# Starting the first layer with memory's keys and values, from inputs turned on the host

## The chip, the cores and the metric

One core of a Trainium2 chip runs the whole program. The time is device microseconds of one execution of the program; the verdict on a kernel is the median of several runs. Inputs are handed over once, ahead of the launch; what the host does to their layout is not in the time.

## What is computed

An encoder of two layers over 512 positions of width 2048, all in float32. Per layer, cut to what matters here:

```python
h = rmsnorm(x, pre_norm_g[l])                       # (512, 2048)
z = h @ w_in[l]                                     # combined input projection, split into columns:
q_lat, kv_lat, k_pe, gb, gc, xin, q_mem, gate = split_cols(z)
...                                                 # latent attention -> a_out, short convolution -> c_out
mem_n = rmsnorm(mem, mem_norm_g[l])                 # (256, 2048), the same mem in both layers
mk, mv = mem_n @ w_mk[l], mem_n @ w_mv[l]           # (256, 512) each: four heads of 128
m_out = softmax(q_mem @ mk^T * scale) @ mv
y = concat(a_out, c_out, m_out) * silu(gate)
x = x + rmsnorm(y @ w_o[l], post_norm_g[l])
```

`rmsnorm(v, g)` is `v * r * g` with one factor `r = (mean(v*v) + eps) ** -0.5` per row (per position, or per memory token) and one gain `g` per column.

## The kernel before

**Products.** Each float32 operand is split into a high half that the matmul format holds exactly and the rest (`split_to`, and `prep` for weights: ScalarE writes the high half, VectorE subtracts it from the source for the low one). `mm3` makes a product of three matmuls: high by high, high by low, low by high. The large projections go by one level of a seven-product scheme (P1 to P7): with the operand halves A11, A12 (token tiles 0 and 1) and A22, S1 to S4, which are made of all four token tiles (0 and 2, or 1 and 3). `left_half` splits A11 and A12 of a token tile; `right_half` puts off, one by one, A22's split and the sums and splits of S1, S2, S4, S3 (`combine`).

**Steps.** `Program` holds a list of steps, each with the weight units it needs. Ahead of a step, `load` issues the units' loads on SyncE's queue (up to eight units ahead, eight raw buffers) and `prep` splits them (two units ahead, three buffers of each half). `defer(cost, fn)` puts work off: every step brings some room, and the queue's head is emitted when its cost is there. `until` empties the queue as far as an operand is needed, all at once. So the program writes one order down, and each engine's instructions stand in that order; in the first part (`manual_schedule`, until `first.close`) VectorE and ScalarE take it literally, behind it the scheduler may reorder these two. TensorE, SyncE and GpSimd keep it throughout.

**Layer 0.** Four tiles of x (128 positions each) are loaded by rows. ScalarE squares and sums (`row_factor`), GpSimd makes the factor, VectorE multiplies it in (`first_rows`), TensorE turns the tile in 16 transposes of 128x128 (`transpose_rows`), and the eviction multiplies the column gain in. Sixty transposes of the identity (`warm`) fill TensorE before. The column gains are loaded by rows and turned with one transpose (`turn_constants`). The first projection group, HEAD, runs in the order P1, P2, P1' and P2' of the second group, P5, P6 with P3, and so on; P1 needs A11, P2 A12, P5 S1. Before P1's second weights come the second halves of the tiles, beside P2 the third and fourth tile.

**Memory in layer 0.** Rows of mem are loaded late in the projection, scaled by their row factor (`mem_rows`) and, in the mixer, turned by 32 transposes (`mem_turn`), split, and written to DRAM as split halves (`mTd`) for layer 1. `mem_steps` makes keys (`mk`, transposed: 128 columns by 256 tokens, four banks) and values (`mv`, tokens by 512 columns, two banks) in eight pairs of steps; the column gain of the memory norm is multiplied into the weights as they are split (`gain`, two pieces of 512 columns). They stand between the gates' transposes; the rotary tables are made beside them.

**Memory in layer 1.** `mem_steps` stands between the transposes at the start of the layer, with the halves reloaded from `mTd` (`mem_reload`); its keys and values go to DRAM and come back for the mixer (`mem_fetch`).

Of the kernel before, what the change touches and what calls it, by code (L numbers as in the profile page):

```python
# [5 lines left out]
F32 = mybir.dt.float32  # L6
F32R = mybir.dt.float32r
# [73 lines left out]
class Program:  # L81
# [36 lines left out]
    def run(self):  # L118
# [39 lines left out]
        def prep(upto):  # L158
            while at["prep"] < min(upto, len(seq)):
# [48 lines left out]
def encoder(tc, x, mem, positions, pre_norm_g, w_in, q_norm_g, w_uq, kv_norm_g, w_ukv, conv_w,  # L208
            mem_norm_g, w_mk, w_mv, w_o, post_norm_g, inv_freq, out):
# [61 lines left out]
    def setup():  # L271
# [11 lines left out]
        nc.scalar.dma_start(rows[2 * n:], conv_w.rearrange("l k (c p) -> (l k c) p", p=P))  # L283
        G["rows"] = rows

    def turn_constants():
        rows = G["rows"]
        n = KT * depth
        m = 2 * n + 12 * depth
        ps = bank("cps")  # L290
        nc.tensor.transpose(ps[:, :m], rows, G["ident"][:m, :m])
        cols = const.tile([P, m], F32, name="cols")
        nc.vector.tensor_copy(cols, ps[:, :m])
# [281 lines left out]
    def row_factor(xt, junk):  # L575
        ssq = small()
        nc.scalar.activation(junk, xt, AF.Square, accum_out=ssq)
        return rsqrt_mean(ssq, D)

    def normalise_rows(xt, dst, on=None):  # L580
        r = row_factor(xt, dst)
        if on is nc.scalar:
            nc.scalar.activation(dst, xt, AF.Copy, scale=r)
        else:
            nc.vector.tensor_scalar_mul(dst, xt, r)
# [29 lines left out]

    def first_load(t):
        xt = G[f"x{t}"] = slab("x")
        nc.sync.dma_start(xt, x[0, t * P:(t + 1) * P, :])

    def first_factor(t):  # L620
        G[f"hs{t}"] = slab("hs")
        G[f"r{t}"] = row_factor(G[f"x{t}"], G[f"hs{t}"])

    def first_rows(t, halves=(0, 1)):
        for h in halves:
            c = slice(h * 1024, (h + 1) * 1024)
            nc.vector.tensor_scalar_mul(G[f"hs{t}"][:, c], G[f"x{t}"][:, c], G[f"r{t}"])
# [820 lines left out]
```

## Time and profile before

| | |
|---|---|
| median of 3 runs | 1506.56 us (1505.59 to 1508.12) |
| span of the profiled execution | 1503.7 us; its own whole time isn't given apart from the runs' |
| TensorE (PE) busy | 1486.0 us, 7613 matmuls and transposes |
| VectorE (DVE) busy | 1082.5 us, 1444 instructions |
| ScalarE (ACT) busy | 873.5 us, 1359 instructions |
| first matmul of a projection | 14.64 us from the span's start |

In the profile's lines a name is that of a tile, `out<-in`; P is a bank of a projection, wh and wl are the halves of a weight unit, wr its raw buffer, A and S the left operands, hs scaled rows, hT a turned tile, mk and mv the banks of keys and values, mH and mL the halves of turned memory. "Lnnn" is the line of the kernel. A time in brackets is what the engine idled ahead of the group, with what ended it. A line of the windows has, for a stretch of the span, its length, the busy time of PE, of its weight loads (PEld), DVE, ACT and GpSimd (POOL), the granted clock, the DMA engines' busy share and GB/s. A line of the groups ends in count, busy us and mean ns of one.

### The profile page before, as it was taken

Reading aid. Unit: us, or ns where it says so; the run is one execution under the profiler, and the core shown is the slowest. Engines: PE = TensorE matmul, PEld = TensorE weight load, DVE = VectorE, ACT = ScalarE, POOL = GpSimd, SP = SyncE. Lnnn points to the kernel's source line nnn. Section 1 sums busy time; section 2 is a strip of 40 time slices with the busy share of each in tenths; the row PEclk is TensorE's granted clock in tenths of the full one; section 3 lists DMA queues with packets and bytes.
Section 4 is the critical chain, followed back from the end, with each engine's and each line's share of the span. In section 5 each row is a group of like instructions: output and inputs, shape, how many; then the busy total and the mean of one; then the engine's idle time right before and its main releaser. Section 6 shows DMA issues by size and latency. Waiting matters only on the chain.

```text
span 1503.7 us, 20253 instructions
## 1 busy us (share of the span) xinstructions
PE 1486.0 (99%) x7613; PEld 1279.1 (85%) x7613; DVE 1082.5 (72%) x1444; ACT 873.5 (58%) x1359; POOL 256.9 (17%) x253
## 2 busy tenths in 40 slices
PE   9999999999999999999999999999999999999997
PEld 7788888988898888888898888888988888988886
DVE  6965776575877668769788765776575486698687
ACT  7743434454767768655688533534464587686443
POOL 1233030322000000230310233030323000003211
PEclk9999999999999999999999999999999999999999
DMA  8999796979582111495987999696979521027945
GB/s 335 216 215 223 192 187 160 203 210 248 168 262 81 56 34 65 101 211 166 319 297 234 236 224 223 196 179 159 212 199 220 152 71 43 29 84 140 257 120 183
DMA packets 142581, 267.19 MB, mean 178 GB/s; under 512 B 17084, under 2 KB 39956, under 8 KB 139156
## 3 DMA queue, kind: packets, MB, share of 16 engines
q0 software_dynamic: 52544, 117.19, 39.7%
q1 hardware_dynamic: 89808, 148.67, 30.0%
q8 instruction: 59, 0.97, 0.3%
q14 instruction: 38, 0.31, 0.1%
q10 hardware_dynamic: 132, 0.05, 0.0%
HBM read 251.20 MB, written 14.68 MB: 177 GB/s over the span
## 4 chain that ended last, share of the span: by engine, by line
PE 93%; ACT 2%; DVE 1%; issue 1%; POOL 1%; DMA 1%; POOLq 0%; DVEq 0%; ACTq 0%
PE P L253 22%; PE P L254 22%; PE P L252 22%; PE ptp L1021 2%; PE tps L772 2%; PE o L253 1%; PE o L254 1%; PE o L252 1%; PE sc L252 1%; PE sc L253 1%; PE sc L254 1%; PE mk L253 1%; PE mk L254 1%; PE mk L252 1%; PE sc L1001 1%
## 5 line engine op out<-in xcount | busy, mean ns | idle before, releaser
L178 DVE TENSOR_TENSOR wl<-wr,wh 128x1024 fp32r<-128x1024 f32 (+1 forms) x400 | 476.9, 1196 | 283.0 <-ACT wh L177 274.5
L177 ACT CAST wh<-wr 128x1024 fp32r<-128x1024 f32 (+1 forms) x400 | 412.6, 1034 | 451.0 <-PE P L254 379.9
L252 PE MATMUL P<-wh,S 128*128 128x512 f32 (+1 forms) x896 | 345.2, 385 | 0.0
L253 PE MATMUL P<-wl,S 128*128 128x512 f32 (+1 forms) x896 | 343.9, 384 | 0.4 <-DVE wl L178 0.4
L254 PE MATMUL P<-wh,S 128*128 128x512 f32 (+1 forms) x896 | 343.3, 383 | 0.0
L252 PE MATMUL P<-wh,A 128*128 128x512 f32 (+1 forms) x656 | 253.1, 386 | 0.2 <-ACT wh L177 0.2
L253 PE MATMUL P<-wl,A 128*128 128x512 f32 (+1 forms) x656 | 251.9, 384 | 0.8 <-DVE wl L178 0.8
L254 PE MATMUL P<-wh,A 128*128 128x512 f32 (+1 forms) x656 | 251.7, 384 | 0.5 <-DVE A L258 0.5
L137 POOL DMA_DIRECT2D wr<-in_w_in_dram x136 | 164.6, 1210 | 460.2 <-DVE wl L178 284.5
L253 PEld LDWEIGHTS P<-wl,S 128*128 128x128 f32 x896 | 168.3, 188 | 30.7 <-DVE wl L178 1.2
L254 PEld LDWEIGHTS P<-wh,S 128*128 128x128 f32 x896 | 168.2, 188 | 30.4
L252 PEld LDWEIGHTS P<-wh,S 128*128 128x128 f32 x896 | 168.1, 188 | 29.6
L254 PEld LDWEIGHTS P<-wh,A 128*128 128x128 f32 x656 | 123.2, 188 | 23.3 <-DVE A L258 1.2
L253 PEld LDWEIGHTS P<-wl,A 128*128 128x128 f32 x656 | 123.2, 188 | 22.8 <-DVE wl L178 1.4
L252 PEld LDWEIGHTS P<-wh,A 128*128 128x128 f32 x656 | 123.1, 188 | 22.3 <-ACT wh L177 0.7
L137 POOL DMA_DIRECT2D wr<-in_w_o_dram x40 | 48.4, 1211 | 530.4 <-DVE wl L178 515.3
L1007 ACT ACTIVATE P<-sc,nm 128x512 f32<-128x512 f32 (+1 forms) x96 | 59.9, 623 | 31.1 <-DVE nm L1004 31.1
L1010 ACT ACTIVATE P<-P,rec 128x512 f32<-128x512 f32 (+1 forms) x96 | 63.2, 661 | 6.7 <-DVE rec L1009 6.7
L1004 DVE TENSOR_REDUCE nm<-sc 128x1 f32<-128x512 f32 (+1 forms) x96 | 57.3, 596 | 9.6 <-PE sc L1002 6.1
L258 DVE TENSOR_TENSOR PT<-ptp,PT 128x512 fp32r<-128x512 f32 (+1 forms) x96 | 55.0, 596 | 10.0 <-ACT PT L257 9.6
L183 DVE SCALAR_TENSOR_TENSOR wl<-wr,cols,wh 128x512 fp32r<-128x512 f32 x64 | 45.9, 750 | 13.5 <-ACT wh L182 13.5
L182 ACT ACTIVATE wh<-wr,cols 128x512 fp32r<-128x512 f32 x64 | 44.0, 726 | 19.2 <-PE mk L253 7.8
(281 smaller groups left out, 2238.7 us busy)
## 6 DMA issues: line engine op xcount, KB each, us to landing
wr<-in_w_in_dram SPq DMA_DIRECT2D x128, 512.0 KB, 5.5
wr<-in_w_in_dram POOLq DMA_DIRECT2D x112, 512.0 KB, 7.3
wr<-in_w_o_dram SPq DMA_DIRECT2D x48, 512.0 KB, 4.0
wr<-in_w_o_dram POOLq DMA_DIRECT2D x40, 512.0 KB, 7.0
wr<-in_w_in_dram SPq DMA_DIRECT2D x32, 416.0 KB, 4.0
wr<-in_w_in_dram POOLq DMA_DIRECT2D x24, 416.0 KB, 5.8
wr<-in_w_mk_dram SPq DMA_DIRECT2D x16, 512.0 KB, 5.7
wr<-in_w_mv_dram SPq DMA_DIRECT2D x16, 512.0 KB, 5.0
```

The costliest lines, as they stand in the source:

```text
L137: engine.dma_start(dst, src, **kw)
L177: nc.scalar.copy(hi[:, :n], src)
L178: nc.vector.tensor_tensor(lo[:, :n], src, hi[:, :n].bitcast(F32), op=ALU.subtract)
L182: nc.scalar.activation(hi[:, h], src[:, h], AF.Copy, scale=g)
L183: nc.vector.scalar_tensor_tensor(lo[:, h], src[:, h], g, hi[:, h].bitcast(F32), op0=ALU.mult, op1=ALU.subtract)
L252: nc.tensor.matmul(ps, ah, bh, start=first, stop=False, **kw)
L253: nc.tensor.matmul(ps, ah, bl, start=False, stop=False, **kw)
L254: nc.tensor.matmul(ps, al, bh, start=False, stop=last, **kw)
L258: nc.vector.tensor_tensor(lo, src, hi.bitcast(F32), op=ALU.subtract)
L1004: nc.vector.tensor_reduce(nmax, ps, axis=AX.X, op=ALU.max, negate=True)
L1007: nc.scalar.activation(pt, ps, AF.Exp, bias=nmax, accum_out=tot)
L1010: nc.scalar.activation(pt, pt, AF.Copy, scale=rec)
```

## The change

The host hands over x and mem a second time, turned (`xt` in tiles of 128 positions, `memt`), and all column gains in one turned table (`columns`). Layer 0 begins with the sixteen memory steps; memory's column gain is multiplied into turned memory as it is split (four pieces of 256 columns a unit), its row factor into keys (along the free side, by a row made with a broadcast and a transpose, `factor_row`) and values (by partition). The same is done in layer 1 with `memt` loaded again. x's rows are still loaded, for the row factors alone (`row_factors`); the turned tiles are scaled in place, sixteen instructions of 128x128 a tile (`turned_scale`). What stands beside which memory step is in `beside`. The third and fourth tile's turned loads come beside memory, their rows beside P2, and their scaling and both `right_half` go on the put-off queue behind P1' has begun. Keys and values of both layers go by DRAM to the mixer, which now is the same in both layers; the rotary tables come in the projection. Sixty warm-up transposes become thirty.

```diff
                 else:
-                    for k, g in enumerate(u.gain()):
-                        h = slice(k * (n // 2), (k + 1) * (n // 2))
+                    gains = u.gain()
+                    for k, g in enumerate(gains):
+                        h = slice(k * (n // len(gains)), (k + 1) * (n // len(gains)))
                         nc.scalar.activation(hi[:, h], src[:, h], AF.Copy, scale=g)
                         nc.vector.scalar_tensor_tensor(lo[:, h], src[:, h], g, hi[:, h].bitcast(F32),
                                                        op0=ALU.mult, op1=ALU.subtract)
...
         G.update(ident=identr.bitcast(F32), identr=identr, mhalf=mhalf, junk=const.tile([P, 512], mybir.dt.bfloat16, name="junk"))
-        rows = scrap("rows", P)[:KT * 2 * depth + 12 * depth]
         n = KT * depth
-        nc.scalar.dma_start(rows[:n], pre_norm_g.rearrange("l (k p) -> (l k) p", p=P))
-        nc.scalar.dma_start(rows[n:2 * n], mem_norm_g.rearrange("l (k p) -> (l k) p", p=P))
...
+        cols = const.tile([P, 2 * n + 12 * depth], F32, name="cols")
+        nc.scalar.dma_start(cols, columns)
...
+    def row_factors(key, src, t, dst):
+
+        def load():
+            G[key, t] = slab("rows")
+            nc.sync.dma_start(G[key, t], src[t * P:(t + 1) * P, :])
+
+        def factor():
+            rows = G.pop((key, t))
+            ssq = small()
+            nc.scalar.activation(rows, rows, AF.Square, accum_out=ssq)
+            ms = small(1, "ms")
+            nc.gpsimd.tensor_scalar(ms, ssq, 1.0 / D, EPS, op0=ALU.mult, op1=ALU.add)
+            nc.gpsimd.tensor_tensor(dst[:, t:t + 1], ms, G["mhalf"][:, :1], op=ALU.pow)
+        return load, factor
+
+    def factor_row(name, ts):
+
+        src = G[name]
+        dst = scrap("row", len(ts) * P)
+        G[name + "_row"] = dst.rearrange("p (t c) -> p t c", c=P)
+        ps = bank("rps")
+        for k, t in enumerate(ts):
+            wide = scrap("wide", P)
+            nc.vector.tensor_copy(wide, src[:, t:t + 1].broadcast_to([P, P]))
+            nc.tensor.transpose(ps[:, k * P:(k + 1) * P], wide, G["ident"])
+        nc.vector.tensor_copy(dst, ps[:, :len(ts) * P])
+
+    def turned_load(t):
+        G[f"hT{t}"] = slab("hT").rearrange("p (k c) -> p k c", c=P)
+        nc.sync.dma_start(G[f"hT{t}"].rearrange("p k c -> p (k c)"), xt[t])
+
+    def turned_scale(t, h):
+        hT, r = G[f"hT{t}"], G["rx_row"][:, t % 2, :]
+        for k in range(8 * h, 8 * h + 8):
+            nc.vector.scalar_tensor_tensor(hT[:, k, :], hT[:, k, :], G["g1_0"][:, k:k + 1], r,
+                                           op0=ALU.mult, op1=ALU.mult)
...
-    def mem_turn(q):
-
-        if q % 4 == 0:
-            G.setdefault("mT", []).append((slab("mH", F32R), slab("mL", F32R)))
-        ps = bank("mps")
-        for j in range(2):
...
     def mem_steps(l):
 
         def unit(name, w, kp):
-            return Unit((name, l, kp), {(name, l, kp): [w[kp * 256:(kp + 1) * 256, :].rearrange("(a p) c -> p a c", p=P)]},
-                        gain=lambda: [G[f"gm_{l}"][:, 2 * kp + a:2 * kp + a + 1] for a in range(2)])
+            return Unit((name, l, kp), {(name, l, kp): [w[kp * 256:(kp + 1) * 256, :].rearrange("(a p) c -> p a c", p=P)]})
+
+        def turned(q):
+            def place():
+                if q % 2 == 0:
+                    G.setdefault("mT", []).append((slab("mH", F32R), slab("mL", F32R)))
+                return tuple(t[:, (q % 2) * 1024:(q % 2 + 1) * 1024] for t in G["mT"][q // 2])
+            return Unit(("mT", l, q), {("mT", l, q): [memt[:, 4 * q:4 * q + 4, :]]}, alloc=place,
+                        gain=lambda: [G[f"gm_{l}"][:, 4 * q + a:4 * q + a + 1] for a in range(4)])
 
         def keys(kp):
-            def f(wk):
+            def f(*ops):
+                wk = ops[-1]
                 if kp == 0:
                     G["mk"] = [bank("mk") for _ in range(4)]
...
                 if kp == 7:
                     km = G["Km"] = slab("Km", F32R).rearrange("p (s i c) -> p s i c", s=2, i=4)
                     for i in range(4):
-                        split_to(km[:, 0, i, :], km[:, 1, i, :], G["mk"][i][:, :MT])
+                        ks = scrap("ks", MT)
+                        nc.vector.tensor_tensor(ks, G["mk"][i][:, :MT], G["rm_row"].rearrange("p t c -> p (t c)"), op=ALU.mult)
+                        split_to(km[:, 0, i, :], km[:, 1, i, :], ks)
...
                 vm = G["Vm"] = slab("Vm", F32R).rearrange("p (s t c) -> p s t c", s=2, t=2)
                 for t in range(2):
-                    split_to(vm[:, 0, t, :], vm[:, 1, t, :], G["mv"][t])
+                    r = G["rm"][:, t:t + 1]
+                    nc.scalar.activation(vm[:, 0, t, :], G["mv"][t], AF.Copy, scale=r)
+                    nc.vector.scalar_tensor_tensor(vm[:, 1, t, :], G["mv"][t], r, vm[:, 0, t, :].bitcast(F32),
+                                                   op0=ALU.mult, op1=ALU.subtract)
...
-                if l > 0:
...
+                for n in ("Km", "Vm"):
+                    d = G[n + "d"] = dram.tile([P, D], F32, name=f"{n}d{l}")
+                    nc.gpsimd.dma_start(d, G.pop(n).rearrange("p a b c -> p (a b c)").bitcast(F32))
...
+        return [s for kp in range(8) for s in ((keys(kp), [turned(kp // 2)] * (kp % 2 == 0) + [unit("mk", w_mk[l], kp)], 0.8),
                                                (values(kp), [unit("mv", w_mv[l], kp)], 0.8))]
...
     def mixer(l, C, gates, pair2, tail):
 
         prods, rot, turn = q_rope_steps(l)
-        if l == 0:
-            ms = [(f, u, 1.0) for f, u, _ in mem_steps(l)]
-            add(tables)
-            add(lambda: pr.defer(3.5, lambda: k_rope(C)))
-            for q in range(8):
-                add(lambda q=q: mem_turn(q))
-                add(gates[q])
-                if q:
-                    put(ms[2 * q - 2:2 * q])
-            put(ms[14:])
-            add(pr.settle)
-            add(k_rope_turn)
-            put(prods)
-        else:
-            add(mem_fetch)
-            put([(g, []) for g in gates[:4]], prods[:1], [(g, []) for g in gates[4:]], prods[1:])
+        add(mem_fetch)
+        put([(g, []) for g in gates[:4]], prods[:1], [(g, []) for g in gates[4:]], prods[1:])
...
-    for t in range(2):
-        add(lambda t=t: first_load(t))
-        add(lambda t=t: first_factor(t))
-        if t == 0:
-            add(lambda: first_rows(0))
-    add(pr.begin_loads(3))
-    add(lambda: first_load(2))
     add(pr.begin_loads(5))
-    add(lambda: first_load(3))
-    add(lambda: warm(60))
-    add(turn_constants)
+    add(lambda: warm(30))
...
+        ms = mem_steps(l)
         if l == 0:
             add(use)
...
-            add(turn_half(0, 0))
-            add(lambda: first_rows(1, (0,)))
-            add(pr.begin_prep(1))
-            add(lambda: left_half(0, (0,)))
-            add(pr.begin_prep(2))
-            add(turn_half(1, 0, nc.scalar))
-            add(lambda: first_rows(1, (1,)))
-            add(lambda: left_half(1, (0,)))
-            add(pr.begin_prep(3))
-            add(lambda: first_factor(2))
-            add(turn_half(0, 1))
+            G.update(rx=const.tile([P, NT], F32, name="rx"), rm=const.tile([P, 2], F32, name="rm"))
+            xr = [row_factors("x", x[0], t, G["rx"]) for t in range(NT)]
+            mr = [row_factors("mem", mem[0], t, G["rm"]) for t in range(2)]
+            scale = [[lambda t=t, h=h: turned_scale(t, h) for h in range(2)] for t in range(NT)]
+            load = [lambda t=t: turned_load(t) for t in range(NT)]
+            left = [[lambda t=t, h=h: left_half(t, (h,)) for h in range(2)] for t in range(2)]
+            beside = {
+                0: [xr[0][0]], 1: [xr[1][0]], 2: [xr[0][1], load[0]], 4: [xr[1][1], load[1]],
+                6: [lambda: factor_row("rx", (0, 1)), mr[0][0]],
+                7: [scale[0][0], mr[1][0]], 8: [left[0][0]], 9: [scale[1][0]], 10: [left[1][0], mr[0][1]],
+                11: [scale[0][1], mr[1][1], load[2]], 12: [left[0][1]], 13: [scale[1][1], load[3],
+                     lambda: factor_row("rm", (0, 1))],
+                14: [left[1][1]],
+            }
+            for n in range(16):
+                put(ms[n:n + 1])
+                for f in beside.get(n, ()):
+                    add(f)
+            add(first.close)
         else:
-            ms = mem_steps(l)
             put(ms[:1])
             add(use)
             for n in range(8):
...
-                if n == 0:
-                    add(lambda: mem_reload(1))
+                if n == 5:
+                    add(lambda: factor_row("rm", (0, 1)))
         (a, b), (a1, b1) = gs[0][:2], gs[1][:2]
         add(owns[0])
+        put(a)
         if l == 0:
-            put(a[:1])
-            add(first.close)
-            add(turn_half(1, 1))
-            add(lambda: left_half(0, (1,)))
-            add(lambda: left_half(1, (1,)))
-            add(lambda: first_rows(2))
-            add(lambda: first_factor(3))
-            add(lambda: first_rows(3))
-            put(a[1:], b[:1])
-            add(turn[2])
-            add(lambda: right_half(0))
-            put(b[1:3])
-            add(turn[3])
-            add(lambda: right_half(1))
-            put(b[3:])
-        else:
-            put(a, b)
+            for t in (2, 3):
+                add(xr[t][0])
+        put(b[:2])
+        if l == 0:
+            for t in (2, 3):
+                add(xr[t][1])
+            add(positions_load)
+        put(b[2:])
         add(owns[1])
-        put(a1, b1)
-        put(*gs[0][2:], *gs[1][2:])
+        put(a1[:1])
+        if l == 0:
+            add(lambda: factor_row("rx", (2, 3)))
+            for t in (2, 3):
+                for h in range(2):
+                    add(lambda t=t, h=h: pr.defer(1.9, scale[t][h]))
+            for t in range(2):
+                add(lambda t=t: pr.defer(0.0, lambda: right_half(t)))
+        put(a1[1:], b1)
+        put(*gs[0][2:])
+        if l == 0:
+            add(tables)
+        put(*gs[1][2:])
+        add(pr.settle)
         add(owns[2])
...
-            add(lambda C=C: k_rope(C))
+        add(lambda C=C: k_rope(C))
         put(g4[8:16])
-        if l == 0:
-            add(mem_load)
...
         put(more[12:])
...
-        if l + 1 < depth:
-            add(lambda: mem_reload(0))
...
+    given.update(
+        x=x, mem=mem, columns=columns, inv_freq=np.array(INV_FREQ, np.float32),
+        xt=x[0].T.reshape(KT, P, NT, P).transpose(2, 1, 0, 3).reshape(NT, P, D),
+        memt=mem[0].T.reshape(KT, P, MT).transpose(1, 0, 2))
```

More of the change, by code (lines that the diff above doesn't have):

```diff
@@ L614, in right_half @@
         combine(left, tt, a[:, :8, :], a[:, 8:, :], b[:, :8, :], b[:, 8:, :])
[L616 to L627, printed above, removed]
     def projection(l):
@@ L1362, in encoder @@
         put(g4[2:8])
-        if l > 0:
-            add(lambda C=C: k_rope(C))
+        add(lambda C=C: k_rope(C))
         put(g4[8:16])
-        if l == 0:
-            add(mem_load)
-            G["mTd"] = dram.tile([4, P, D], F32, name="mTd")
-        lat = [latent_turn(l, "cq", j) for j in range(4)] + [latent_turn(l, "ckv", j) for j in range(2)] + [k_rope_turn] * (l > 0)
+        lat = [latent_turn(l, "cq", j) for j in range(4)] + [latent_turn(l, "ckv", j) for j in range(2)] + [k_rope_turn]
         gm = lambda t, C=C: C["gm"][:, t, :]
         more = [(f, []) for f in lat + [qm_turn(j, C) for j in range(4)] + [gate_turn(12 + j, gm, j) for j in range(4)]]
-        if l == 0:
-            more.insert(8, (mem_rows, []))
         put(weave(g4[16:], more[:12], 2, 2))
```

73 lines of the change are left out of this document (12 added, 61 removed).

## Prediction

> **What bounds the kernel now.** I read the page first (span, engines, chain), then the list of what TensorE waited for, then the first 50 us as a timeline, and last the groups of like instructions, for the prices.
>
> ```profile
> span 1503.7 us, 20253 instructions
> PE 1486.0 (99%) x7613; PEld 1279.1 (85%) x7613; DVE 1082.5 (72%) x1444; ACT 873.5 (58%) x1359; POOL 256.9 (17%) x253
> ...
> PE 93%; ACT 2%; DVE 1%; issue 1%; POOL 1%; DMA 1%; POOLq 0%; DVEq 0%; ACTq 0%
> ```
>
> TensorE (PE) is busy 99% of the span and holds 93% of the chain. So each us of PE work taken away is a us of time, and so is each us that PE is made to wait; the other engines count only where PE ends up waiting for them. The profiled span (1503.7 us) is 2.9 us under the median of the three runs (1506.56). I make the sum on the span and carry the difference over to the median. This measurement can tell about 0.2% (3.0 us) from no change.
>
> ```profile
> PE hps L596 <- DVE hs L627: 1.6, 1, 1.6
> PE P L253 <- DVE wl L178: 1.2, 2, 0.8
> PE sc L252 <- DVE rm L904: 0.8, 2, 0.4
> ...
> PE P L254 <- DVE A L258: 0.5, 1, 0.5
> PE mk L253 <- DVE mL L258: 0.4, 1, 0.4
> ...
> PE P L252 <- ACT wh L177: 0.2, 1, 0.2
> ```
>
> Behind the start, only the waits for wl, A, wh and mL are tied to work that moves: 2.3 us in five waits. A 128x512 matmul is recorded as 0.39 us but the next starts 0.227 us later (below), so each wait has another 0.16 us hidden in the recorded busy time: 3.1 us of waits that the change can take away. The waits in the attention part (sc for rm) come twice, once per layer, although only layer 0 has memory steps ahead of it; so taking these steps away there changes nothing in them.
>
> **The start.**
>
> ```profile
> 0.73 0.86 SPq L618 DMA_DIRECT2D x<-in_x_dram  x2
> 1.61 8.74 PE L1253 MATMUL warm<-identr 128*128 128x128 f32 x60 [1.61 <-DVE identr L275]
> 2.32 1.28 ACT L577 ACT_TABLE_LOAD   x1 [2.32 <-issue]
> 6.26 1.92 ACT L577 ACTIVATE hs<-x 128x2048 f32<-128x2048 f32 x1 [2.66 <-DMA x<-in_x_dram]
> 8.94 1.93 ACT L577 ACTIVATE hs<-x 128x2048 f32<-128x2048 f32 x1 [0.68 <-DMA x<-in_x_dram]
> 10.86 1.03 ACT L177 CAST wh<-wr 128x1024 fp32r<-128x1024 f32 x1
> 14.64 0.48 PE L252 MATMUL P<-wh,A 128*128 128x512 f32 x1
> ...
> 5.00:7.00 2.00, 2.00 (x17) 2.00 (x16) 0.00 (x0) 0.74 (x1) 0.00 (x0) 1.00 1.00 414
> 7.00:9.00 2.00, 2.00 (x21) 2.00 (x20) 0.00 (x0) 1.32 (x3) 0.55 (x2) 1.00 0.98 393
> ```
>
> The two x tiles (1.05 MB each) are used at 6.26 and 8.94 us: 2.68 us a MB, which is the 390 to 414 GB/s of the windows. So loads land one after the other, at 3.6 us + bytes / 0.395 MB per us. The first real matmul is at 14.64 us.
>
> In the changed kernel the first load is the turned memory (0.52 MB, lands at 4.9), then mk's first weights (6.2). The built program has ScalarE (ACT) wait for the memory tile before its table load (1.28), which before ran under the wait: 6.2. Then four scaled pieces of 256 columns.
>
> ```profile
> L1010 ACT ACTIVATE P<-P,rec 128x256 f32<-128x256 f32 x32 | 16.5, 523 | 0.0
> L257 ACT CAST Km<-mk 128x256 fp32r<-128x256 f32 x8 | 2.9, 385 | 0.5 <-PE mk L254 0.3
> L818 DVE SCALAR_TENSOR_TENSOR lat<-lat,r,growk 128x256 f32<-128x256 f32 x8 | 3.5, 480 | 0.0
> L258 DVE TENSOR_TENSOR Km<-mk,Km 128x256 fp32r<-128x256 f32 x8 | 2.9, 419 | 0.0
> L329 DVE TENSOR_TENSOR ropescr<-ropescr 128x128 f32<-128x128 f32 x10 | 2.9, 291 | 0.3
> ...
> 30.40 3.49 DVE L178 TENSOR_TENSOR wl<-wr,wh 128x1024 fp32r<-128x1024 f32 x3
> ```
>
> Three 1024-wide splits on VectorE (DVE) take 3.49 us, each recorded 0.09 longer than its step: 1.135 us a piece. With that overlap taken off, a 256-wide scaled piece costs 0.40 on both engines, and a 128-wide product of two tensors 0.20; there are 64 of the latter, the scaling of the turned x, with a column factor besides. I take 0.22; bounds 0.20 (full overlap) and 0.32 (none). The four pieces end at 7.8, the cast of the weights (1.05) at 8.9: **first matmul at 9.0 instead of 14.64, -5.6 us**. The third needs the low half of the weights (another 1.2): +1.0.
>
> Of the warm-up's 60 transposes 30 stay. 60 take 8.74 us, while warm ones take 0.109 each (next fence): 1.61 + 8.74 is 19 or 20 at twice the step, to 5.7 us, and 40 at 0.109. Thirty end at 6.8, and PE then idles for 2.2 us. I price that at nothing: before, too, PE idled ahead of its first matmuls (the 1.6 us wait for hs) and they kept full pace. The Trainium skill (TensorE: Matmul & The Clock Gate, part 1) says that the array runs at half clock until a window of about 3.4 us was busy, and falls back after an idle one. By that rule, too, 2.2 us of idling lose nothing.
>
> **PE work that goes.**
>
> ```profile
> 24.95 0.39 PE L253 MATMUL P<-wl,A 128*128 128x512 f32 x1
> ...
> 27.22 0.39 PE L254 MATMUL P<-wh,A 128*128 128x512 f32 x1
> ...
> 30.34 1.75 PE hps L596 x16
> 407.77 0.44 PE mps L701 x4
> 408.21 0.44 PE tps L772 x4
> 414.27 0.44 PE mps L701 x4
> ```
>
> Sixteen transposes take 1.75 us: 0.109 each. From 24.95 to 27.22 lie ten matmuls: 0.227 each, so 2.72 a projection step of twelve. From one mps to the next is 6.50 us with eight transposes (0.88) in it: 5.62 for a step of keys (2.9) and one of values (2.7), 45 us for all sixteen steps, the same wherever they stand. Layer 0 loses 64 transposes of x (24 of them ahead of 14.64, in the start term already) and 32 of memory, and eight come for the factor rows: 40 + 32 - 8 = 64 x 0.109 = **-7.0 us**.
>
> **New waits in the memory stage.** The order of each engine's instructions is fixed in the built program, and ACT and DVE take theirs in order.
> - Ten half-MB loads stand on SP's queue ahead of x's first tile: 6.3 MB, 19.5 us. Its square (1.92) stands on ACT ahead of the cast for the third pair's weights, which had landed at 12.9: cast done at 22.6. PE has two pairs (11.2 us, from 10.0) to do until 21.2. +1.4, and +1.0 for the low half: **+2.4**.
> - PE comes to the transposes of x's factor at 32.3; DVE goes on behind them at 32.9 with eleven 1024-wide splits (12.5), four scalings of eight (7.0) and four narrow pieces (1.6), 21.1 us, and waits 1.4 for a cast that stands behind the square of memory's first tile on ACT. Only then (55.4) comes the copy that memory's factor needs. PE has one step of values and three pairs, 19.6 us, to 51.9: **+3.5**.
> - At the end each of four key tiles goes DVE, ACT, DVE before the next (0.33 + 0.38 + 0.33 and some 0.25 of handing over: 1.3). The split of P1's second weights stands on DVE behind that of the first (1.1), all four tiles (5.2) and an A12 split (1.1, and 0.6 waiting for its cast); with its own 1.2 that is 9.2 us, begun 0.4 after PE goes on. PE has 2.9 + 2.7 + 1.4 = 7.0: **+2.6**.
>
> **The large one, ahead of P5.** x's third and fourth tile are now loaded and scaled behind P2, and `right_half` is put off behind four scalings of price 1.9. The steps of P1' and P2' give room for about these scalings; the rest comes off the queue in one go when P5 first asks for it.
> - DVE from the factor row to S1 of token tile 0: 32 narrow scalings (7.0), eight weight splits (9.1), a split of A22, a difference and S1's low half (3.4), two 512-wide sums (1.2), some 1.7 waiting for casts: 22.4. PE has seven steps, 19.1: +3.3.
> - In the built program ten more 1024-wide operations stand on DVE between S1 of tile 0 and S1 of tile 1 (S2, S4, S3 of tile 0 with their sums, tile 1's A22): 11.4 + 0.6 for four results waited for = 12.0. PE has tile 0's products of one step, 1.4: +10.6.
>
> Together **+13.9**.
>
> ```profile
> 43.14 1.22 DVE L258 TENSOR_TENSOR S<-hT,S 128x1024 fp32r<-128x1024 f32 x1
> ...
> 63.13 1.22 DVE L258 TENSOR_TENSOR S<-hT,S 128x1024 fp32r<-128x1024 f32 x1
> 64.27 1.22 DVE L178 TENSOR_TENSOR wl<-wr,wh 128x1024 fp32r<-128x1024 f32 x1
> ```
>
> Before, DVE split the first S at 43 us and S1 of tile 1 at 63 us, one at a time between weight splits, and no wait of P for S stands in the list above. So nothing like this price is paid now.
>
> **Layer 1.** The memory operand is loaded and split anew: sixteen 256-wide pieces on DVE and ACT (6.4 us on each) amid residuals and norms, against 2 us saved on plain weight splits. Bounds 0 (DVE is not full) and 6; I take **+2.6**, where PE has to wait for a split twice.
>
> **At nothing.** Layer 0's keys and values go to DRAM and back 330 us later; 4 MB of reloads go and 2 MB of loads come; one more table load (1.28) falls into the projection, where ACT idles 42%.
>
> Sum: -5.6 - 7.0 - 3.1 (old waits) + 1.0 + 2.4 + 3.5 + 2.6 + 13.9 + 2.6 = **+10.3**. Span 1514.0, median 1506.56 + 10.3 = 1517.
>
> **Rivals.**
> - *The second half is ready in time* (faster): DVE works S1 of both tiles in before P5. It is busy 72%, so room exists. Then the 13.9 go: -3.6, 1503.0. Against it: nothing can move on DVE's queue any more. It needs the ten operations to take under 1.4 us. Chance 0.05. If the layer-1 wait is also partly there, or half of the 13.9, the time lies within 0.2% of before: 0.06.
> - *Narrow scalings are not overlapped* (0.32 instead of 0.22): 64 x 0.10 = 6.4 us more on DVE, some 5 of them ahead of a waiting PE: 1522. For it: a factor column and a tensor in one instruction, in place. 0.10.
> - *Transfers bind the memory stage*: 16.8 MB must be in for its last weights. At 395 GB/s that is 46 us, against use at 59. At 300 GB/s it would be 60, and x's first tile would land at 24.6 instead of 19.5: +5, 1522. Against it: the windows above hold 390 and more. 0.05.
> - *The clock falls back* in the idle time ahead of 9.0: about 4 us of matmuls at half pace, +2, 1519. 0.04.
>
> **How the numbers follow.** The forecast, 1517, holds with 0.70: the waits ahead of P5 are counted in whole instructions. Its own range is 1512 to 1520. The range reaches down to a half-size P5 wait (1509) and up to the dear scalings (1523). Slower by over 0.2% has 0.89, within 0.2% 0.06, faster 0.05.
>
> **What would show it.** Right: first mk matmul near 9 us; a wait of about 10 us of P for S by DVE near 112 to 123 us, the longest of the run; rps waiting for wide near 55. Wrong: no wait over 4 us ahead of P5, or PE's idle time under 25 us in all.

## The result, and the profile after

The changed kernel takes 1522.73 us (median of four runs, 1520.69 to 1524.05), the kernel before 1507.33 us in the same comparison: a ratio of 1.0103, 95% interval 1.0088 to 1.0117, or 15.4 us more. The prediction said +10.3 and 1517, range 1509 to 1523. The profiled run is the longest of the four, 1524.05 us with a span of 1522.3; against the span before (1503.7) that is +18.6. So some 3 us of the difference between the two traces belong to these two executions and not to the change: this one is 1.3 above its median, and 1503.7 is a short span for the kernel before, whose 49 later runs have 1502.7 to 1508.4, median 1505.0.

The page of the changed kernel: span, engines, chain of waits.

```profile
span 1522.3 us, 20025 instructions
PE 1484.2 (98%) x7494; PEld 1273.7 (84%) x7494; DVE 1095.7 (72%) x1503; ACT 864.1 (57%) x1312; POOL 256.4 (17%) x249
...
PE 83%; DVE 5%; issue 3%; ACT 3%; DMA 2%; POOL 2%; POOLq 0%; DVEq 0%; SPq 0%; ACTq 0%
```

PE runs 119 instructions fewer than before, at 0.109 each 13.0 us less work (30 warm-up transposes, 24 of x ahead of the first matmul, 64 net, one for the gains). Yet its busy time fell by only 1.8, and its share of the chain from 93% to 83%. So two things must be found: waits, and work that takes longer than it did. What PE waited for in the changed kernel (total, times, longest):

```profile
PE P L253 <- ACT S L258: 8.6, 2, 8.4
PE mk L255 <- DVE wl L178: 3.3, 4, 1.2
PE rps L588 <- DVE wide L587: 2.9, 1, 2.9
PE P L255 <- DVE S L259: 2.8, 1, 2.8
PE mk L253 <- ACT wh L177: 2.7, 3, 1.6
PE P L254 <- DVE wl L178: 2.2, 3, 0.8
...
PE hps L610 <- DVE row L589: 0.9, 1, 0.9
```

The waits of P for S, absent before, are the largest. Here they are on PE's timeline (start, duration, in brackets the idle time ahead), with the first matmul of keys, and the matmul at 130.20, where full pace is back:

```profile
9.44 0.38 PE L253 MATMUL mk<-mH,wh 128*128 128x256 f32 x1 [1.56 <-ACT wh L177]
...
110.37 0.40 PE L254 MATMUL P<-wl,S 128*128 128x512 f32 x1
113.55 0.79 PE L255 MATMUL P<-wh,S 128*128 128x512 f32 x1 [2.78 <-DVE S L259]
...
114.99 0.63 PE L255 MATMUL P<-wh,S 128*128 128x512 f32 x1
124.02 0.79 PE L253 MATMUL P<-wh,S 128*128 128x512 f32 x1 [8.40 <-ACT S L258]
124.61 0.63 PE L254 MATMUL P<-wl,S 128*128 128x512 f32 x1
125.34 0.79 PE L255 MATMUL P<-wh,S 128*128 128x512 f32 x1
...
130.20 0.40 PE L254 MATMUL P<-wl,S 128*128 128x512 f32 x1
```

and the instructions of VectorE behind them:

```profile
102.15 2.20 DVE L598 SCALAR_TENSOR_TENSOR hT<-hT,cols,row 128x128 f32<-128x128 f32 x8
...
112.25 1.24 DVE L259 TENSOR_TENSOR S<-hT,S 128x1024 fp32r<-128x1024 f32 x1
...
124.07 1.22 DVE L259 TENSOR_TENSOR S<-hT,S 128x1024 fp32r<-128x1024 f32 x1
```

From one start to the next, less one step of 0.23, PE stood 2.95 and 8.80 us. S1's low half of tile 1 starts 11.8 us behind that of tile 0, with nine operations of 1024 between (ten steps of 1.14, the forecast's count, and some waiting). ACT, which the list names for the long wait, is the cast of that S1, and it waited for VectorE's difference. That is the wait that was forecast (12.0 between the two, 13.9 us in all), in its place.

The work that takes longer shows in the windows. The columns are length, busy time of PE, PEld, DVE, ACT and POOL, the granted clock, DMA share, GB/s:

```profile
7.33:10.74 3.41, 1.09 (x8) 0.64 (x6) 2.96 (x6) 3.41 (x6) 0.00 (x0) 1.00 1.06 405
10.74:14.15 3.41, 3.41 (x16) 3.41 (x17) 2.18 (x2) 0.54 (x1) 0.00 (x0) 0.50 1.04 387
...
58.53:61.94 3.41, 3.41 (x18) 3.41 (x18) 2.47 (x6) 0.81 (x2) 0.00 (x0) 0.50 0.96 327
...
113.14:130.21 17.07, 8.16 (x18) 5.47 (x19) 16.76 (x15) 7.02 (x7) 1.19 (x1) 0.50 0.42 77
795.81:799.22 3.41, 1.59 (x11) 1.38 (x12) 3.40 (x5) 3.41 (x5) 0.56 (x1) 1.00 0.59 160
799.22:802.63 3.41, 3.41 (x19) 3.41 (x18) 2.45 (x2) 2.54 (x4) 0.00 (x0) 0.50 0.91 255
```

Four stretches at a clock of 0.50, none of which the kernel before has between its start and its end. In them a 128x512 matmul starts 0.43 us behind the last instead of 0.23. Up to 125.34 that costs nothing: this matmul waits for S1's low half in any case, which VectorE has at 125.29 (124.07 + 1.22). From 125.34 to 130.20 stand eleven starts. They take 4.86 us, where full pace needs 2.6 (0.34 for the first behind a wait, as from 110.03 to 110.37 ahead of the stretch, and ten of 0.227): 2.2 us that no wait hides.

Where the change lies is read from the first scores of the mixer (the tile view of QmH: count, shortest, median and longest duration in ns, first and last start). Before, and after:

```profile
L252 PE MATMUL sc<-Km,QmH x32: 277/323/387, 463.9 to 1231.4; 128*128 128x256 f32 x32
```

```profile
L253 PE MATMUL sc<-Km,QmH x32: 277/323/389, 475.1 to 1248.8; 128*128 128x256 f32 x32
```

Up to there the changed kernel has lost 11.2 us (forecast 10.3 - 2.6 = 7.7), from there to the end of the span 1047.2 against 1039.8, 7.4 more (forecast 2.6). Of the two together some 3 us are these executions' own.

### The profile page after: what moved, and what is told of

It reads as the page before. It is cut to its first block, busy times and chain, and to the rows that moved or that the text cites. A ratio compares the mean times of both kernels' runs of the same rounds, so it can differ in the third digit from the quotient of the medians.

```text
span 1522.3 us, 20025 instructions
## 1 busy us (share of the span) xinstructions
PE 1484.2 (98%) x7494; PEld 1273.7 (84%) x7494; DVE 1095.7 (72%) x1503; ACT 864.1 (57%) x1312; POOL 256.4 (17%) x249
## 4 chain that ended last, share of the span: by engine, by line
PE 83%; DVE 5%; issue 3%; ACT 3%; DMA 2%; POOL 2%; POOLq 0%; DVEq 0%; SPq 0%; ACTq 0%
PE P L254 20%; PE P L255 20%; PE P L253 20%; PE ptp L1000 2%; POOL wr L137 2%; PE tps L751 2%; DVE wl L178 2%; DMA wr<-in_w_o_dram 1%; PE o L254 1%; PE o L255 1%; PE o L253 1%; PE sc L253 1%; PE sc L254 1%; PE sc L255 1%; PE sc L980 1%
## 5 line engine op out<-in xcount | busy, mean ns | idle before, releaser
L178 DVE TENSOR_TENSOR wl<-wr,wh 128x1024 fp32r<-128x1024 f32 (+1 forms) x432 | 515.4, 1198 | 294.5 <-ACT wh L177 285.7
L177 ACT CAST wh<-wr 128x1024 fp32r<-128x1024 f32 (+1 forms) x432 | 444.1, 1032 | 481.3 <-PE P L255 383.6
L258 ACT CAST PT<-ptp 128x512 fp32r<-128x512 f32 (+1 forms) x96 | 46.4, 522 | 6.3 <-DVE S L259 3.2
L1000 PE MATMUL ptp<-identr,P 128*128 128x128 f32 x320 | 46.4, 274 | 0.7 <-ACT P L986 0.7
```

The source lines that it names most:

```text
L177: nc.scalar.copy(hi[:, :n], src)
L178: nc.vector.tensor_tensor(lo[:, :n], src, hi[:, :n].bitcast(F32), op=ALU.subtract)
L258: nc.scalar.copy(hi, src)
L1000: nc.tensor.transpose(ps[:, k * P:(k + 1) * P], pt[:, k * P:(k + 1) * P], G["ident"])
```

## The experiments

Each kernel is compared with the kernel before on the same chip. Times are medians; the changed kernel's is 1522.7. The kernel before took 1506.3 to 1507.3 in the four comparisons, so between runs of different ones a difference of 1 us says nothing.

**The clock: junk work in the waits.** First only in the two waits of P5:

```diff
 def products(q, c, tt, ops):
     hi, lo = ...
+    if c == 0 and q == "P5" and passes is HEAD and key == (0, 0):
+        bk_ = bank("warm")
+        for k in range(26 if tt == 0 else 76):
+            nc.tensor.transpose(bk_[:, (k % 4) * P:(k % 4 + 1) * P], G["ident"], G["ident"])
     pr.until(lambda: left.there(LEFT[q], 2 * c, tt))
```

> The changed kernel with 102 junk transposes of the identity (26 and 76) put on TensorE just ahead of P5's products for token tile 0 and 1, in the two waits of 3.2 and 9.0 us. At 0.109 us each they end before the operands come, so the waits stay as they are; only the array is kept busy in them. Theory A (the waits alone cost): nothing changes, 1522.7 us. Theory B (the array falls to half clock behind the waits; the trace shows it at 0.50 from 113.1 to 130.2 us, with 1.5 us of matmuls ahead of the second wait and 6 us behind it at half pace): about 3.5 us less, 1519.2, and no stretch at 0.50 between 113 and 130. Rival C (the junk delays the operands or is itself too long): slower than 1523.

Measured 1520.5 (1518.8 to 1522.0; ratio 1.0089, 1.0076 to 1.0102). Windows of this run:

```profile
113.14:126.37 13.23, 11.33 (x88) 10.01 (x87) 13.09 (x12) 5.04 (x5) 1.05 (x1) 1.00 0.52 94
126.37:129.78 3.41, 3.41 (x10) 2.63 (x9) 3.28 (x4) 1.99 (x2) 0.04 (x1) 0.50 0.00 0
```

The stretch of 17.07 us at half clock shrank to 3.41. So the idle time did cause it, as theory B has it; but what is left (1.9 us of P waiting for S behind the junk, in three waits) still set off one such stretch, so only part of the 2.2 us came back: the same eleven starts take 4.2 us (125.55 to 129.73), 0.7 less. The first scores came 0.4 us sooner than in the changed kernel's trace. The rest of the 2.3 us between the medians is not shown to be the junk's (1.7 of it may be the missing stretch at 799), and the two intervals overlap. That the clock fell because PE stood idle is shown; its price behind P5 is read from the trace, and only the 0.4 to 0.7 us were won back by a run.

Then in all long waits (besides the above, the warm-up 48 instead of 30, `warm(27)` ahead of memory's factor row, `warm(9)` ahead of layer 1's first keys):

> As the run before, with junk transposes in the other long waits too: the warm-up is 48 instead of 30 (to about 8.8 us), 27 ahead of memory's factor row (the wait of 54 to 57 us), and 9 ahead of layer 1's first keys. Every operand's way is unchanged. Theory A (waits alone): 1522.7. Theory B (half clock): the four stretches at 0.50 of the profiled run (at 10.7, 58.5, 113.1 and 799 us) held 1.7, 1.7, 3.5 to 3.8 and 1.7 us of lost pace, 8.6 to 8.9 in all, against the profiled 1524.05: 1515 to 1516, with a mean clock near that of the kernel before (0.998). The layer 1 part is the least sure, since the wait for the low weights behind its first two matmuls can't be filled.

Measured 1522.8 (ratio 1.0101, 1.0087 to 1.0116): nothing gained, though the mean clock rose from 0.989 to 0.995. PE's timeline and the windows say why:

```profile
23.95 0.39 PE L253 MATMUL mk<-mH,wh 128*128 128x256 f32 x1 [2.01 <-ACT wh L177]
24.17 0.28 PE L254 MATMUL mk<-mL,wh 128*128 128x256 f32 x1
25.21 0.58 PE L255 MATMUL mk<-mH,wl 128*128 128x256 f32 x1 [0.76 <-DVE wl L178]
```

```profile
10.71:14.15 3.44, 3.44 (x26) 3.31 (x27) 2.19 (x2) 1.22 (x2) 0.00 (x0) 1.00 1.04 388
...
24.37:31.20 6.83, 6.07 (x26) 5.80 (x26) 3.09 (x4) 4.43 (x6) 0.74 (x2) 0.50 1.04 403
```

From 10.7 to 14.15 the clock is full now, PE reaches the third pair 1.5 us sooner (its last product of values starts at 21.55 instead of 23.1), and waits longer there: that cast stands on ScalarE behind the square of x's first tile, whose rows landed 1.0 us later in this trace (the square starts at 20.96, there at 19.97). Then the clock falls behind this wait instead, for 6.83 us, and once more at 72.16 for 3.41. The 27 junk transposes ahead of memory's factor row did fill its wait: they end when wide comes (61.1), and the clock stays full there. But VectorE comes to wide 3.6 us later than in the changed kernel (60.77, there 57.13), about what the half clock from 24.37 (3.4 lost) took; the first scores are 3.0 later (478.1). So theory B's sum was wrong: pace lost ahead of a wait that another engine sets costs nothing, filling one wait moved the fall behind the next, and the stretches can't be added up. The plainest sign of the first is the low product of the third pair: it starts at 24.23 in the changed kernel, with half clock from 10.74, and at 24.24 in the next run, with full clock there.

**P5: sooner, or only in another order.** The second half's rows, factors and scalings sooner, and the two tiles' put-off work in turn:

```diff
-    14: [left[1][1]],
+    14: [left[1][1], xr[2][0]], 15: [xr[3][0]],
 ...
-put(a); rows of tiles 2, 3; put(b[:2]); factors; put(b[2:]); put(a1[:1]); factor row; scalings (1.9 each)
+put(a[:1]); factor 2; put(a[1:2]); factor 3; put(a[2:]); factor row; scalings (1.6 each); put(b); put(a1, b1)
 ...
-for t in range(2): pr.defer(0.0, lambda: right_half(t))
+pr.defer(0.0, lambda: right_halves(1.1))   # A22, difference, S1 of both tiles, then S2 of both, S4, S3
```

> The changed kernel with the second half of x made ready sooner: rows of the third and fourth tile loaded beside memory's last steps instead of behind P1, their squares beside P1, the factor row and the scalings ahead of P2 instead of behind P1', and A22, S1, S2, S4, S3 of the two token tiles put off in turn instead of all of tile 0 before tile 1. The same instructions, in another order. Theory A (the wait of P5 alone): the 12.2 us that TensorE waits there go: 1510.5. Theory B (with the clock's loss behind it): 12.2 + 3.5 less, 1507. Rival C (the work of VectorE is what binds, so the wait turns up at S2 and S4 of P6 and P3): at least half of it comes back, 1515 to 1517.

Measured 1508.3 (ratio 1.0009, 1.0001 to 1.0018): 14.4 us less, between theories A and B and nearer to B. PE no longer waits in P5, no stretch at half clock follows there (one of 6.83 stands at 56.8, at memory's factor row), and one wait of 1.5 us for S, in the pass of P6 and P3, is new. First scores:

```profile
L253 PE MATMUL sc<-Km,QmH x32: 277/323/387, 461.0 to 1231.5; 128*128 128x256 f32 x32
```

This kernel reaches the mixer 2.9 us ahead of the kernel before (463.9) and loses that, and more, behind it. The same instructions as in the changed kernel, 14.1 us sooner: most of the slowdown comes from how late the second half of x is squared, scaled and split. The order of the ten operations alone:

```diff
-for t in range(2): pr.defer(0.0, lambda: right_half(t))
+pr.defer(0.0, both)   # A22, difference, S1 of tile 0, then of tile 1, then S2, S4, S3 of tile 0, of tile 1
```

> The changed kernel with one edit: of the put-off work, S1 of token tile 1 stands ahead of S2, S4 and S3 of token tile 0 instead of behind them. Nothing is loaded or scaled sooner. Between the two S1 then stand A22's split, a difference and S1 itself, 3.4 us of VectorE and a cast instead of 12, against 1.4 us of products. Theory A (the order of these ten operations is what cost 10.6 us): the second wait falls from 9.0 to some 2.5 us, nothing else moves, 1515 with the clock's share. Theory B (VectorE has that much to do ahead of P6 and P3 in any order; only work begun sooner helps): the 7 us taken from P5 come back as waits for S2 and S4, 1520 to 1522.

Measured 1522.5 (ratio 1.0107, 1.0093 to 1.0120): theory B, half a us past its range. PE's waits in P5, and later in P6:

```profile
118.05 0.79 PE L253 MATMUL P<-wh,S 128*128 128x512 f32 x1 [4.39 <-ACT S L258]
...
120.38 0.80 PE L255 MATMUL P<-wh,S 128*128 128x512 f32 x1 [1.11 <-DVE S L259]
...
134.32 0.50 PE L253 MATMUL P<-wh,S 128*128 128x512 f32 x1 [1.67 <-ACT S L258]
136.75 0.50 PE L255 MATMUL P<-wh,S 128*128 128x512 f32 x1 [1.70 <-DVE S L259]
```

The long wait halves, and S2 is late in its place. VectorE is busy 19.8 of the 20 us from 110 to 130 in the changed kernel; in another order it has as much to do. Of the two edits only the one that begins work sooner helped.

**The memory stage.**

```diff
+nc.scalar.activation(G["junk"][:, :1], mhalf[:, :1], AF.Copy, scale=mhalf[:, 1:2])   # in setup: loads the table
-warm(30)
+warm(45)
-2: [xr[0][1], load[0]],  ...  13: [scale[1][1], load[3], factor_row("rm")]
+2: [load[0]], 3: [xr[0][1]],  ...  13: [factor_row("rm"), scale[1][1], load[3]]
-for i in range(4): ks = product; cast; subtraction
+ks[0], cast 0; then for each i: ks[i + 1], cast i + 1, subtraction i
```

> The changed kernel with four edits in the memory stage, the second half of x left as it is: a one-column scaled copy makes ScalarE load its table before memory lands; the warm-up is 45 transposes; x's first square stands one step later, memory's factor row ahead of the last scaling instead of behind it; the four key tiles go through VectorE and ScalarE in a pipeline (the next product ahead of the last subtraction) instead of one after the other. Theory A (each wait was a cost of its own, as the prediction summed them): the waits of about 2.4 (wh of the third pair, with its low half), 2 of the 2.9 for wide, 1 of the key chain and 1.3 of table load go: 1516. Theory B (the stage is bound by what lands and by VectorE as a whole, so that what one wait loses the next gets, as the run with junk in all waits showed: its earlier start came back as a 2.4 us wait at 24 us): 1520 to 1522.

Measured 1518.7 (ratio 1.0080, 1.0067 to 1.0093): 4.0 us less, between the theories. In its list of waits:

```profile
PE mk L255 <- DVE wl L178: 2.7, 3, 1.2
PE mk L253 <- ACT wh L177: 1.8, 3, 0.8
...
PE P L253 <- ACT wh L177: 1.3, 1, 1.3
PE P L254 <- DVE wl L178: 1.3, 2, 0.9
...
PE rps L589 <- DVE wide L588: 0.8, 1, 0.8
```

The wait for wide fell from 2.9 to 0.8 and the third pair's are gone, but P1's first weights are now waited for (wh 1.3 at 62.84, where the changed kernel has no wait), and the clock falls at 64.28 for 3.41 us. So memory's factor row comes 3.4 us sooner than in the changed kernel (54.11 for 57.50), the first wait of P5 ends 1.5 sooner (112.01), and the first scores come 1.0 sooner (474.1): most came back. The other 3 of the 4.0 us stand behind the first scores in the traces, where these edits touch little; what made them isn't shown.

**Layer 1.** The row factor kept:

```diff
-if n == 5: factor_row("rm", (0, 1))          # layer 1
+if n == 5: scrap tile <- DRAM, where layer 0 wrote the row
```

> The changed kernel with memory's row factor written to DRAM in layer 0 and read back in layer 1, instead of made there again by two broadcasts, two transposes and a copy. The prediction put layer 1's whole 2.6 us on splitting memory anew; the trace shows 0.9 us of hps waiting for row in layer 1, and two transposes (0.2). If that is a cost: 1.1 us less, 1521.6. If it is hidden or comes back (the put-off work of VectorE binds): 1522.7.

Measured 1521.5 (ratio 1.0096, 1.0082 to 1.0110), 1.2 us less where 1.1 were expected, but within the scatter, so neither theory is excluded; the wait of hps for row is gone from the trace. And the memory operand reloaded as before:

```diff
-Unit(turned memory, gain=...)   in both layers;  weights plain
+Unit(turned memory) in layer 0 only, halves written to mTd and reloaded in layer 1;  weights with gain=...
```

> The changed kernel with layer 1's memory operand as before: layer 0 splits turned memory without a gain, writes the halves to DRAM, layer 1 reloads them, and the column gain is multiplied into the weights as they are split (two pieces of 512) in both layers. The row factor stays on keys and values. It prices splitting memory anew in layer 1. The prediction's 2.6 us: 1520.1. The trace's reading (waits for wh and wl of 2.7 us at 796 to 799 and 1.7 us at half clock behind them): 1518.3. Rival (it is the factor row in layer 1, which stays, that costs): 1522. In layer 0 plain memory splits make the first matmul earlier by some 1.5 us and the scaled weight pieces make the later memory steps slower; I take these as even.

Measured 1522.2 (ratio 1.0100, 1.0087 to 1.0113): no gain in all, but the parts differ. First scores:

```profile
L253 PE MATMUL sc<-Km,QmH x32: 278/323/389, 478.5 to 1247.0; 128*128 128x256 f32 x32
```

From there to its end (1519.5) are 1041.0 us: 1.2 more than before, where the two junk and early runs above that keep the new layer 1 have 3.5 to 4.4 more (1518.9 - 474.7; 1504.3 - 461.0) and the changed kernel's own profile 7.4. So splitting memory anew costs 2.3 to 3.2 us by these traces. They are single executions that scatter by some us; but all nine that split anew have 1043.0 to 1047.2, and the other one with the reload, below, 1041.1. Layer 0 is 3.4 us later than in the changed kernel. The third pair is waited for 3.6 us, but that wait is not the loss: the pair starts at 23.41, in the changed kernel at 23.32, since its cast stands behind x's square in both. The loss comes behind it: half clock from 24.01 to 27.42 (1.7 us), and memory's factor row at 60.09 instead of 57.50. How much of it is the gain on sixteen weight units instead of four of memory, and how much the halves written to DRAM, was not taken apart.

**All together.**

> The edits of the runs on the second half of x, on the memory stage and on layer 1's row together. With the second half early alone it was 1508.3. Theory A (waits add up): 1508.3 - 6.5 - 1.1 = 1500.7, some 6 us under the kernel before. Theory B (the memory stage is bound as a whole): 1506 to 1508.

Measured 1506.4 (ratio 0.9992, 0.9982 to 1.0002), no difference from the kernel before, as theory B has it: the 4.0 and 1.2 us of the two runs above came to 1.9 on top of the early second half. With the reload:

> The run before with layer 1's memory operand reloaded as split halves and the gain on the weights in both layers, as in the run that did this alone. There layer 1 took 1031.1 us from the first scores of the mixer in layer 0 to the end, against 1033.1 to 1037.2 in the other three and 1029.9 before, and layer 0 lost 3.3 us up to that point, with a wait of 4 us for the third pair's weights behind x's square. If that loss was the square's place (here it stands a step later), this is 2 us faster than the run before; if it was the price of scaling weights on ScalarE and VectorE, 1 us slower.

(The times in this text count from a scores matmul 10 us behind the first.) Measured 1514.2 (ratio 1.0049, 1.0036 to 1.0061), neither. What ScalarE waited for between 60 and 90 us, and the window in question:

```profile
ACT rows L577 <- DMA rows<-in_x_dram: 10.4, 1, 10.4
```

```profile
60.00:70.00 10.00, 9.06 (x43) 7.39 (x42) 9.06 (x16) 5.55 (x9) 1.06 (x2) 0.93 1.04 418
70.00:80.00 10.00, 4.36 (x20) 3.27 (x18) 0.00 (x0) 1.52 (x1) 0.00 (x0) 0.92 1.01 417
```

The 4.2 MB of halves written to DRAM are 10 us of work (at the row's 0.42 MB per us) for DMA engines that are full, with a share over 1.00, until 80 us; the third tile's rows land that much later, ScalarE's square waits for them, and P's weights stand behind it (7.1 us of PE). That it is the writes that delay the rows is read from one trace and was not tested apart. This is the rival "transfers bind the memory stage", at a place and with bytes that the changed kernel does not have.

**A faster version.** To the kernel with all edits (row kept, no reload) come the low halves of weights last:

```diff
-for j in range(2): high*high, high*low, low*high          # left operand by weights
+for j in range(2): high*high, low*high
+for j in range(2): high*low                               # the ones that need wl
```

(likewise keys and values), A12 of tile 1 split beside P1, and the scalings one step later at 1.3 each.

> The run with all edits, and three more: in each group of products the matmuls that need the low half of a weight unit come last (for keys all eight banks' high products first), since waits of 1.0 to 1.5 us for wl stand behind every late cast; A12 of token tile 1 is split beside P1 instead of ahead of it; the scalings of the second half are put off one step later at a lower price. That run (1506.4) still showed 2.7 us of mk and 2.2 us of P waiting for wl, 1.3 for wh ahead of P1, 1.6 for S, and 3.4 us at half clock twice. If these waits are costs of their own: 1500 to 1502, faster than the kernel before by 0.3%. If they come back elsewhere: 1505 to 1506.

Measured 1502.3 (1501.9 to 1504.9, seven runs), ratio 0.9972, 0.9961 to 0.9983: faster than both kernels. Its waits (the profiled run is the slowest of the seven):

```profile
PE rps L597 <- DVE wide L596: 3.1, 2, 2.2
PE mk L742 <- ACT wh L177: 2.6, 3, 1.4
PE P L520 <- DVE S L259: 1.7, 1, 1.7
```

The same order in the kernel before:

> The kernel before with only that order of the matmuls (low halves of weights last). It tells how much of the run before is owed to an edit that has nothing to do with the change. Its waits for wl and mL are 2.1 us in six places in the trace: 1505 if they go, 1506.8 if they were hidden.

Measured 1507.5 (ratio 1.0007, 0.9998 to 1.0016): nothing. The waits for wl are gone from its trace, and one of 2.2 us for wh, near 950, is new. So the gain of the run before isn't this order's alone. Which of its three edits pays was not tested; its first scores come at 459.6, in the run with all edits at 459.4, so the traces don't show the gain in layer 0, and where it arises stays open.

## Why the prediction came out as it did

The direction and the mechanism were right, by its own steps; the sum was 5.1 us short. The measured 1522.7 lies 0.3 us inside the range and outside the forecast's own 1512 to 1520. The upper end had been set at 1523 for dear scalings, 0.32 us apart; they start 0.26 apart. So that the time fell inside the range is in part luck: other terms, below, carried it there.

- **Start**, first matmul at 9.0: 9.44.
- **PE work**, -7.0 with the start's and the warm-up's transposes apart: the counts hold.
- **Memory stage.** The third pair's +2.4: where the clock did not fall at 10.7 (the run with the second half early) the first and third matmul of that pair start 1.52 and 1.04 us behind the ones before them instead of 0.23 and 0.12: 2.2. Memory's factor row, +3.5: 3.33 - 0.23 = 3.1. Ahead of P1's second weights, +2.6: 0.9 in this trace, with 1.7 of half clock just ahead (58.53 to 61.94) that took the rest of it. Not foreseen: waits for wh and wl of a keys unit at 47 and 48 us, 1.4 together.
- **Old waits**, -3.1: one of the five, 0.4 us for wl, stands behind the first scores, where nothing was moved; 2.5 go ahead of them.
- **P5**, +13.9: from 110.37 to 130.20 stand 18 starts, 4.1 us at full pace, so 15.7 are lost. 2.2 of it is the half clock behind the last wait; 13.5 are the waits, with the half clock between them, which they took up. Its place, its cause and the 12 us between the two S1 held; the term was 0.4 too high, although the narrow scalings start 0.26 apart ((2.20 - 0.35) / 7, where 0.35 is the length of one) and not 0.22.
- **The clock** is the step that failed, and the largest miss. The prediction priced idle time ahead of the first matmuls at nothing, and set the rival of a fall only there. The clock did fall there, at 10.74, with 1.09 us of PE in the 3.41 before. That loss was swallowed by the next wait. But it fell behind P5's wait too, where nothing came to swallow it: 2.2 us that no term held.
- **Layer 1**, +2.6, bounds 0 to 6: 3.5 and 4.4 in the two traces above that share its layer 1. The two waits for a split are there, 0.8 and 1.2 us at 796 and 798; what no step counted is the wait for the factor row (0.9). The changed kernel's own profile has 1.7 us of half clock at 799 besides, and 1.9 us of waits of P for weights near 690 and 1434; the run with the second half early has none of these, the one with the order alone 1.8.

Up to the first scores the terms as measured add up: -5.2 - 7.0 - 2.5 + 0.9 (the third matmul) + 2.2 + 3.1 + 2.6 + 1.4 + 15.7 = 11.2, the 11.2 of the two traces. So 3.5 of the 5.1 us arise there. The rest, 1.6, is layer 1, if the way to the first scores is alike in every execution (475.1 here, 475.0 in the run with the order alone).

Of the signs that the prediction named, the longest wait (P for S, 8.4 us to 124), the wait of rps for wide near 55 (54.2 to 57.5) and PE's idle time (1522.3 - 1484.2 = 38 us) came as it said.

What stays open: how much of the 2.2 us behind P5 is lost in an average run, since the junk kept one stretch of it and the runs scatter by 3 us; and the price of layer 1 to better than 1 us.

## What to carry to other kernels

A queue of put-off work that is emptied at its first user turns into one long wait, and another order inside it only moves that wait; begin its inputs sooner, and look which engine is full over the whole stretch. Behind each forecast wait (here two of about 1 us close together were enough), ask whether the matmuls that follow run at half clock, and whether another wait takes that loss up. A saving ahead of a wait that another engine or the DMA sets is worth nothing, so price waits in a row as one chain, not one by one.

## What the runs showed of the hardware

The stretches at a clock of 0.50 are whole multiples of 3.41 us (3.41, 6.83, 17.07), and whether a wait sets one off depends on where it falls: the same two waits ahead of layer 1's keys (0.8 and 1.2 us) lost the clock at 799 in one trace and kept it in the run with junk in P5. What decides shows when a grid of 3.41 us is laid through the clock's changes in all thirteen traces: the clock fell behind each of the 34 windows at full clock with under 1.45 us of PE's recorded work, behind 7 of the 14 with 1.45 to 1.9, and behind none with more. In the run that kept it the two waits stood in two windows, with 2.7 and 2.2 us of work. The Trainium skill (TensorE: Matmul & The Clock Gate, part 1) says that windows of this length run freely, and lets the clock fall after an idle one. The length agrees; but the window ahead of 799.22 had 1.59 us of matmuls in it (the row 795.81:799.22), around two waits of about 1 us each, so the window need not be idle throughout; here the measurement decides. The same holds for the prediction's 2.2 us of idling, which by that rule lose nothing: the window ahead of 10.74 had 1.09 us of work, and the clock fell. Behind P5 the stretch went on for 6.2 us after the wait's end: the window from 123.38 had 2.7 us of work at half clock and didn't end it, the next, a full one, did.
